# Staging the weight sums of a seven-product up-projection, with new priorities for evictions, squares and residual steps

## The chip, the cores and the metric

The kernel runs on one NeuronCore of a Trainium2 chip. The metric is the device time of one execution in microseconds (us). TensorE (PE in the profile) multiplies, VectorE (DVE), ScalarE (ACT) and GpSimd (POOL) do elementwise work, and SyncE's queue (SP) issues the DMAs. Each engine runs its own queue in order: an instruction that waits holds back everything behind it on the same engine.

## The reference, cut to what matters

The computation is a trunk of two layers, a gated DeltaNet and an mLSTM mixer, each followed by a causal convolutional feed-forward block (ConvFFN). There are 1040 tokens of width 1024 (16 learned meta tokens ahead of 1024 frames). Every sub-layer is normed before and after and is added to the residual stream:

```python
def conv_ffn(h, w_up, conv_w, conv_b, w_down):
    u = causal_depthwise_conv(h @ w_up, conv_w) + conv_b
    gate, up = u[..., :FFN_DIM], u[..., FFN_DIM:]
    return (jax.nn.silu(gate) * up) @ w_down
...
for i in range(DEPTH):
    a_in = rms_norm(hs, norm_w[i, 0])
    mix = gated_deltanet(a_in, ...) if i % 2 == 0 else mlstm(a_in, ...)
    hs = hs + keep * rms_norm(mix, norm_w[i, 1])
    f = conv_ffn(rms_norm(hs, norm_w[i, 2]), ffn_w_up[i], ffn_conv_w[i], ffn_conv_b[i], ffn_w_down[i])
    hs = hs + keep * rms_norm(f, norm_w[i, 3])
```

All is float32. FFN_DIM is 2816, that is 22 column tiles of 128 for the gate and 22 for the up half.

## The kernel before, in words

**Precision.** Every large product is made of three fast matmuls (`mm3`, lines 233 to 235): a weight is split into a high and a low part, and so is the activation, and high·high, high·low and low·high are accumulated. The split of one weight tile of 128x512 (`split_slot`, line 129) is a cast on ACT (line 137) and a subtraction on POOL (line 138). Split weights live in ten slots of the tag `w`, so in five pairs; raw weights in nine slots of the tag `raw`.

**Tokens.** The 1040 tokens are two halves of 520 (`t`), each of two quarters of 260 (`n`).

**The up-projection** (`up`, line 1238) works on one tile `j` at a time: 128 gate columns and 128 up columns. It has two forms.
- Plain (four weight tiles, `plain`, line 180): for the first half of the tokens, for j from 0 to 5. Four groups of 24 matmuls; each result is copied out of PSUM by ACT (line 1250).
- Seven products (`quad`, line 162): the 2x2 block product (two row blocks of the weight by two column blocks; two quarters of tokens) in the Strassen-Winograd form. Seven products of 12 matmuls take the place of eight. The weight side needs four sums of 128x512 tiles on DVE: s1 (line 171), s3 (line 174), s2 (line 175), s4 (line 177). s2 overwrites the raw tile of a11, and s4 that of s2, so each must wait until the split before it has been read by POOL. The seven weights are used in the order a11, s2, s3, s1, s4, a22, a12. After each product `combine` (line 194) folds the PSUM bank into temporaries and results: an ACT copy for product 0 (line 203), DVE adds for the others (line 196, by the profile), which free the bank.

The order of tiles (`ffn_plan`, line 1285) is: six plain tiles for the first half; then j = 6 to 11 for both halves ("pair" tiles, 14 products), each followed by tile j - 6 for the second half alone ("single" tiles, 7 products); then j = 12 to 21 as pairs. After a tile's products, the causal convolution (ACT line 1276, DVE line 1278), the SiLU (ACT line 1280), the gate product (POOL line 1281) and a store follow.

**Weights ahead.** `next_quad` (line 187) is called at the start of each tile. It loads and prepares the next tile's weights (as long as fewer than seven weight tiles are ready ahead), then hands over the current tile's. So the whole of `quad` for tile T+1, its four DMAs, four sums and seven splits, is issued ahead of the products of tile T.

**Norms and residual.** A down or output projection (`second`, line 386) accumulates in SBUF (DVE lines 439 and 441) and, in its last group, sums squares over the features (`squares`, line 284: ACT line 294, DVE line 295). `post` (line 334) then loads the old residual stream, norms the result (a matmul with ones on PE, line 302, and Ln and Exp on ACT, lines 262 and 265), scales it (DVE line 352), adds it to the stream (DVE line 353), stores it, and sums the squares for the next norm. It is put off by `later` and run by `tick`, that is after a set amount of PE work. The norm's matmul keeps its program place on PE. `ffn_operands` (line 1183) then scales the new stream (DVE line 1206) and makes the activation side of the seven products (casts on ACT line 1212, DVE lines 1213 and 1217).

**What sets the order.** The builder orders each engine's queue when the program is compiled. What is issued earlier in the program has precedence; `high_priority(300)` gives an instruction the precedence of one issued 300 instructions earlier; an ordering edge (`order`) forces one instruction behind another on its engine. Before the change, `combine` and the accumulations have 300 (the accumulations of a last group 3000), and the copies of plain tiles, the squares and `post` have nothing.

Of the kernel before, what the change touches and what calls it, by code (L numbers as in the profile page):

```python
# [12 lines left out]
ALU = mybir.AluOpType  # L13
# [16 lines left out]
QB = HB // 2  # L30
# [2 lines left out]
N_RAW, N_SPLIT = 9, 10  # L33

W_AHEAD = 7

N_PAGES = 19

# [4 lines left out]
LAG_POST, LAG_N, LAG_PRE, LAG_OPS = 6, 6, 16, 2  # L43

LAST = ("f1", 1)
# [31 lines left out]
def run(g):  # L77
    for _ in g:
        pass


class Trunk:
# [5 lines left out]
    def page(self, tag, name, bufs, dt=F32):  # L88
        return self.pool.tile([P, BS], dt, tag=tag, name=name, bufs=bufs)
# [72 lines left out]
    def quad(self, src, name):  # L162

        a11, a21, a22, a12, s1 = [self.raw_slot(f"{name}_{i}") for i in range(5)]
        for t, q in ((a21, 2), (a22, 3), (a11, 0), (a12, 1)):
            self.nc.sync.dma_start(t, src(q))
        v = self.nc.vector
        split = lambda t, n: self.split_slot(t, f"{name}_{n}")  # L170
        v.tensor_tensor(s1, a21, a22, ALU.add)
        w = [split(a11, "a11")]
        s3, s2, s4 = a21, a11, a11
        v.tensor_tensor(s3, a11, a21, ALU.subtract)
        v.tensor_tensor(s2, s1, a11, ALU.subtract)
        w += [split(s2, "s2"), split(s3, "s3"), split(s1, "s1")]
        v.tensor_tensor(s4, a12, s2, ALU.subtract)
        return w + [split(s4, "s4"), split(a22, "a22"), split(a12, "a12")]

    def plain(self, src, name):  # L180

# [4 lines left out]

    def next_quad(self):

        while self.quads and (not self.ready or sum(len(w) for w in self.ready[1:]) < W_AHEAD):
            make, *args = self.quads.pop(0)  # L190
            self.ready.append(make(*args))
        return self.ready.pop(0)

    def combine(self, i, ps, tmp, out):

        add = lambda o, u: self.nc.vector.tensor_tensor(o, ps[:, :QB], u, ALU.add)  # L196
        m1, u2, u3 = tmp
        with self.tc.high_priority(300):
            self.combine_now(i, ps, add, m1, u2, u3, out)

    def combine_now(self, i, ps, add, m1, u2, u3, out):
        if i == 0:
            self.nc.scalar.copy(m1, ps[:, :QB])
        elif i == 1:
            add(u2, m1)
        elif i == 2:
            add(u3, u2)
        elif i == 3:
            add(out[3], u3)
            add(u2, u2)  # L210
        elif i == 4:
            add(out[1], u2)
        elif i == 5:
            add(out[2], u3)
        else:
            add(out[0], m1)

    def temps(self, name):
        return [self.page(tag, f"{n}_{name}", 2)[:, :QB] for n, tag in (("m1", "part"), ("u2", "rs"), ("u3", "sum"))]
# [63 lines left out]

    def squares(self, pages, name, acc=None):

        nc = self.nc
        n = pages[0].shape[1]
        for m, p in enumerate(pages):
            if acc is None:
                acc = self.page("sum", f"ss_{name}", 2)[:, :n]  # L290
                nc.scalar.activation(acc, p, AF.Square)
                continue
            sq = self.scratch(f"sq_{name}_{m}")[:, :n]
            self.last_square = nc.scalar.activation(sq, p, AF.Square)  # L294
            nc.vector.tensor_tensor(acc, acc, sq, ALU.add)  # L295
        return acc
# [37 lines left out]
    def post(self, t, n, acc, mix, post, pre, name, direct, then):  # L334


        nc = self.nc
        q = 2 * t + n
        sl = slice(q * QB, (q + 1) * QB)
        old, src, rt = self.hs, self.new_hs, self.new_rt  # L340

        def job():
            hs = []
            c = 4 if name[0] == "f" or t == 0 else 2
            for g in range(KD // c):
                h = self.fp_page(f"hs_{name}_{q}_{g}") if c == 4 else self.raw_input(f"hs_{name}_{q}_{g}")
                nc.sync.dma_start(h, old[:, c * g : c * g + c, sl])
                hs.append(h)
            page = lambda m: hs[m // c][:, m % c]
            r = self.norm(acc, f"o{name}{q}")  # L350
            for m in range(KD):
                nc.vector.scalar_tensor_tensor(mix[m], mix[m], self.nw[:, post, m : m + 1], r, ALU.mult, ALU.mult)  # L352
                (nc.gpsimd if pre is None and m % 2 else nc.vector).tensor_tensor(page(m), page(m), mix[m], ALU.add)  # L353
                if direct:
                    self.put_input(page(m), m, sl)
            if pre is None:
                t0 = max(NMETA - q * QB, 0)
                o0 = q * QB + t0 - NMETA
                out = self.a["out"].rearrange("(m p) t -> p m t", p=P)
                for m in range(0, KD, 2):  # L360
                    nc.sync.dma_start(out[:, m : m + 2, o0 : o0 + QB - t0], hs[m // c][:, m % c : m % c + 2, t0:])
                return
            for g, h in enumerate(hs):
                nc.sync.dma_start(src[:, c * g : c * g + c, sl], h)
            acc2 = self.squares([page(m) for m in range(KD)], f"{name}{q}")

            def factors():
                self.norm(acc2, f"{name}{q}", rt[:, sl])
                if then:
                    self.later(LAG_OPS, lambda: then(src, rt))  # L370

            self.later(LAG_PRE, factors)

        self.later(LAG_POST + (0 if (name, t) == LAST else n * LAG_N), job)

    def next_stream(self, name, pre):

# [860 lines left out]
    def up(self, L, j, halves):  # L1238

        nc = self.nc  # L1240
        w = self.next_quad()
        tmp = {t: self.temps(f"u{L}_{j}_{t}") for t in halves if len(w) == 7}
        u = {(t, i, n): self.page("C", f"u_{L}_{j}_{t}_{i}_{n}", N_PAGES) for t in halves for n in range(2) for i in range(2)}
        if len(w) == 4:
            for h in range(2):
                for n in range(2):
                    ps = self.next_bank(f"up_{L}_{j}_{h}_{n}")[:, :QB]
                    for k in range(KD):
                        self.mm3(ps, [z[:, k % 4] for z in w[2 * h + k // 4]], self.xplain(k, n), k == 0, k == KD - 1)
                    nc.scalar.copy(u[0, h, n][:, 2 : 2 + QB], ps)  # L1250
                    self.tick(4)
        for i in range(7) if len(w) == 7 else ():
            for t in halves:
                ps = self.next_bank(f"up_{L}_{j}_{t}_{i}")
                for k in range(4):
                    self.mm3(ps[:, :QB], [z[:, k] for z in w[i]], self.xo[t](i, k), k == 0, k == 3)
                self.combine(i, ps, tmp[t], [u[t, h, n][:, 2 : 2 + QB] for h in range(2) for n in range(2)])
                self.tick(2)
        for t in halves:
            y = {}  # L1260
            for n in range(2):
                for h in range(2):
                    p = u[t, h, n]
                    if t + n == 0:
                        nc.gpsimd.memset(p[:, :2], 0.0)
                    elif n == 0 and len(halves) == 1:
                        nc.gpsimd.tensor_copy(p[:, :2], self.ftail[:, j, h])
                    else:
                        nc.gpsimd.tensor_copy(p[:, :2], u[t - (1 - n), h, 1 - n][:, QB : QB + 2])
                    if t == 0 and n == 1 and len(halves) == 1:  # L1270
                        nc.gpsimd.tensor_copy(self.ftail[:, j, h], p[:, QB : QB + 2])
                    y[h] = self.page("C", f"y_{L}_{j}_{t}_{h}_{n}", N_PAGES)[:, :QB]
                    tt = h * NF + j
                    taps = self.fcw[:, tt, :]
                    z = self.bank(("pp", "px")[h], f"z_{L}_{j}_{t}_{h}_{n}")[:, :QB]
                    nc.scalar.activation(z, p[:, 2 : 2 + QB], AF.Identity, scale=taps[:, 2:3], bias=self.fcb[:, tt : tt + 1])  # L1276
                    for i in (1, 0):
                        nc.vector.scalar_tensor_tensor(z if i or not h else y[h], p[:, i : i + QB], taps[:, i : i + 1], z, ALU.mult, ALU.add)  # L1278
                    if h == 0:
                        nc.scalar.activation(y[0], z, AF.Silu)  # L1280
                nc.gpsimd.tensor_tensor(y[0], y[0], y[1], ALU.mult)
                c0 = t * HB + n * QB
                nc.sync.dma_start(self.hidden[:, j, c0 : c0 + QB], y[0])
# [214 lines left out]
```

## Time and profile before

| | us |
|---|---|
| median of 3 runs (3446.24 to 3463.75) | 3447.37 |
| the profiled execution, device time | 3444.23 |
| span of its instructions | 3442.5 |
| PE busy | 3212.2 |
| DVE busy | 2373.1 |
| POOL busy | 1652.2 |
| ACT busy | 1609.0 |

The span is the time from the first to the last instruction; the device time has 1.7 us around it. Busy times are unions over the span. PE's clock is also read in the profile: the share of full speed that was granted to it, 0.969 over the whole span. A matmul's end is modelled, so where PE is busy all the time it may still wait for nothing but its own pipeline. In the waits view, a row names the waiting engine and line, what it waited for, the total in us, how often, and the longest.

By the views over stretches, the gated DeltaNet and most of its output projection take the first 1290 us, the plain tiles of the first ConvFFN begin at 1353 us, the seven-product tiles run from 1461 to 1865 us and the down-projection until about 2150 us; in the second ConvFFN the plain tiles begin at 2649 us and the seven-product tiles run from 2755 to 3162 us.

### The profile page before, as it was taken

The page shows a single profiled execution, that of the slowest core. Times are in us where ns is not written, and L with a number is a line of the kernel's source. Part 1 is how long each engine was busy: PE and PEld are TensorE (multiplying, and loading weights), DVE is VectorE, ACT ScalarE, POOL GpSimd, SP SyncE. Part 2 cuts the span into 40 slices and gives each one's busy share as a digit, 9 for nine tenths or more (in the row PEclk, how much of TensorE's full clock was granted, in tenths as well). Part 3 has the DMA queues.
Part 4 walks back from the last instruction along what each step waited for, and adds up shares of the span by engine and source line. Part 5 has one row for each costly group of instructions (what it writes and reads, how often), then busy time and mean ns, then how long its engine had stood idle before and what let it go on. Part 6 is the DMA issues. An engine that isn't in the chain of part 4 may idle for free. (4 is left out here: it accounts for less than half of the span.)

```text
span 3442.5 us, 68429 instructions
## 1 busy us (share of the span) xinstructions
PE 3212.2 (93%) x25368; PEld 3119.6 (91%) x25368; DVE 2373.1 (69%) x5143; ACT 1609.0 (47%) x3390; POOL 1652.2 (48%) x1890
## 2 busy tenths in 40 slices
PE   7999999999999998799999989899998799999998
PEld 6889988988988897799999989899998799999998
DVE  7777777777767649877677484534469867777474
ACT  5455545555545435655455243323345645445232
POOL 2433443444334444577665434333344477666453
PEclk9999999999999999899999999999999899999999
DMA  3011100101001344422224453211125422224452
GB/s 118 23 37 34 34 29 31 34 32 34 31 31 40 107 132 152 134 93 93 78 78 133 133 182 125 93 44 50 56 78 183 136 90 87 87 75 132 132 180 88
DMA packets 234511, 297.75 MB, mean 86 GB/s; under 512 B 20684, under 2 KB 167104, under 8 KB 234176
## 3 DMA queue, kind: packets, MB, share of 16 engines
q1 hardware_dynamic: 234176, 293.37, 26.3%
q8 instruction: 200, 3.28, 0.4%
q14 instruction: 135, 1.11, 0.1%
HBM read 240.06 MB, written 53.23 MB: 85 GB/s over the span
## 5 line engine op out<-in xcount | busy, mean ns | idle before, releaser
L233 PE MATMUL pj_gi<-xh_in,wh_gi 128*128 128x348 f32 x1152 | 394.2, 342 | 5.5 <-ACT wh_gi L137 3.7
L233 PE MATMUL dn_f<-so_f,wh_f 128*128 128x260 f32 x1344 | 386.6, 288 | 11.8 <-ACT wh_f L137 5.0
L235 PE MATMUL pj_gi<-xh_in,wl_gi 128*128 128x348 f32 x1152 | 395.7, 343 | 0.9 <-POOL wl_gi L138 0.9
L234 PE MATMUL pj_gi<-xl_in,wh_gi 128*128 128x348 f32 x1152 | 393.5, 342 | 0.0
L235 PE MATMUL dn_f<-so_f,wl_f 128*128 128x260 f32 x1344 | 384.7, 286 | 0.0
L234 PE MATMUL dn_f<-so_f,wh_f 128*128 128x260 f32 x1344 | 384.5, 286 | 0.0
L138 POOL TENSOR_TENSOR wl_f<-wr_f,wh_f 128x512 fp32r<-128x512 f32 x168 | 226.0, 1362 | 246.0 <-ACT wh_f L137 113.5
L1278 DVE SCALAR_TENSOR_TENSOR z<-u,fcw,z 128x260 f32<-128x260 f32 x528 | 243.4, 487 | 49.8 <-ACT z L1276 35.0
L138 POOL TENSOR_TENSOR wl_u_s<-wr_u,wh_u_s 128x512 fp32r<-128x512 f32 x176 | 228.2, 1300 | 97.7 <-ACT wh_u_s L137 97.3
L233 PEld LDWEIGHTS dn_f<-so_f,wh_f 128*128 128x128 f32 x1344 | 257.7, 192 | 13.6 <-ACT z L1276 5.5
L441 DVE TENSOR_TENSOR acc_f<-acc_f,dn_f 128x260 f32<-128x260 f32 x320 | 133.1, 421 | 189.2 <-PE dn_f L235 188.2
L234 PEld LDWEIGHTS dn_f<-so_f,wh_f 128*128 128x128 f32 x1344 | 258.2, 192 | 0.2
L235 PEld LDWEIGHTS dn_f<-so_f,wl_f 128*128 128x128 f32 x1344 | 258.2, 192 | 0.1
L1276 ACT ACTIVATE z<-u,fcb,fcw 128x260 f32<-128x260 f32 x352 | 192.3, 570 | 93.7 <-DVE u L196 92.4
L233 PEld LDWEIGHTS pj_gi<-xh_in,wh_gi 128*128 128x128 f32 x1152 | 222.1, 193 | 8.0 <-ACT wh_gi L137 4.0
L235 PEld LDWEIGHTS pj_gi<-xh_in,wl_gi 128*128 128x128 f32 x1152 | 222.6, 193 | 2.4 <-POOL wl_gi L138 1.2
L234 PEld LDWEIGHTS pj_gi<-xl_in,wh_gi 128*128 128x128 f32 x1152 | 222.2, 193 | 0.7 <-issue 0.2
L138 POOL TENSOR_TENSOR wl_gi<-wr_gi,wh_gi 128x512 fp32r<-128x512 f32 x96 | 132.4, 1380 | 157.8 <-ACT wh_gi L137 153.8
L137 ACT CAST wh_u_s<-wr_u 128x512 fp32r<-128x512 f32 x176 | 105.9, 615 | 192.5 <-PE up L234 134.9
L697 DVE SCALAR_TENSOR_TENSOR gy<-u_g,c_gdn_conv_w_g,gy 128x348 f32<-128x348 f32 x288 | 187.9, 663 | 7.9 <-ACT gy L695 5.4
L138 POOL TENSOR_TENSOR wl_u_a<-wr_u,wh_u_a 128x512 fp32r<-128x512 f32 x132 | 170.1, 1293 | 37.0 <-ACT wh_u_a L137 36.3
L137 ACT CAST wh_f<-wr_f 128x512 fp32r<-128x512 f32 x168 | 103.1, 617 | 178.8 <-PE dn_f L234 133.0
(501 smaller groups left out, 11718.0 us busy)
## 6 DMA issues: line engine op xcount, KB each, us to landing
wr_u<-in_ffn_w_up_dram SPq DMA_DIRECT2D x224, 256.0 KB, 2.6
wr_f<-in_ffn_w_down_dram SPq DMA_DIRECT2D x176, 256.0 KB, 2.8
wr_gi<-in_gdn_w_in_dram SPq DMA_DIRECT2D x96, 256.0 KB, 2.6
h<-y SPq DMA_DIRECT2D x176, 130.0 KB, 2.3
si_f<-h SPq DMA_DIRECT2D x88, 260.0 KB, 3.5
wr_go<-in_gdn_w_out_dram SPq DMA_DIRECT2D x64, 256.0 KB, 2.7
wr_mi<-in_ml_w_in_dram SPq DMA_DIRECT2D x44, 256.0 KB, 2.6
o_g<-gy SPq DMA_DIRECT2D x48, 174.0 KB, 1.8
```

The source lines that it names most:

```text
L137: nc.scalar.copy(hi, part(raw))
L138: nc.gpsimd.tensor_tensor(lo, part(raw), hi.bitcast(F32), ALU.subtract)
L233: nc.tensor.matmul(out, w[0], x[0], start=start, stop=False)
L234: nc.tensor.matmul(out, w[0], x[1], start=False, stop=False)
L235: nc.tensor.matmul(out, w[1], x[0], start=False, stop=stop)
L441: nc.vector.tensor_tensor(acc[m][n], acc[m][n], ps, ALU.add)
L697: ins = nc.vector.scalar_tensor_tensor(y, u[:, j : j + BS], taps[:, j : j + 1], y, ALU.mult, ALU.add)
L1276: nc.scalar.activation(z, p[:, 2 : 2 + QB], AF.Identity, scale=taps[:, 2:3], bias=self.fcb[:, tt : tt + 1])
L1278: nc.vector.scalar_tensor_tensor(z if i or not h else y[h], p[:, i : i + QB], taps[:, i : i + 1], z, ALU.mult, ALU.add)
```

## The change: what it does, and its diff

Four things change.
- **`quad` in stages.** The first part still comes at the start of tile T, ahead of its products: the four loads, s1, s3 and the split of a11. The second (s2 and the splits of s2, s3, s1) is issued after product 3 of tile T, the third (s4 and the splits of s4, a22, a12) after product 5. Both sums get an ordering edge behind the last `combine` of that product. In a plain tile the stages are issued after its first and its second column block, without an edge. `next_quad` issues whatever is left before it hands a tile over, and counts an unfinished quad as seven weight tiles.
- **Plain copies** (line 1250) get `high_priority(300)`.
- **`squares`** gets `high_priority(300)` wherever it is called.
- **`post`'s job** gets `high_priority(300)`: its loads, norm, scaling, adds, stores and squares. (The squares inside it thereby have both offsets.) The later job, the norm for the next sub-layer, has none.

`combine` now returns its last instruction; what it computes, and in which order, is the same. Products, sums, splits and loads are the same in number and size.

```diff
+S2_BEHIND, S4_BEHIND = 3, 5
...
 def quad(self, src, name):
...
         split = lambda t, n: self.split_slot(t, f"{name}_{n}")
+        s3, s2, s4 = a21, a11, a11
         v.tensor_tensor(s1, a21, a22, ALU.add)
-        w = [split(a11, "a11")]
-        s3, s2, s4 = a21, a11, a11
         v.tensor_tensor(s3, a11, a21, ALU.subtract)
-        v.tensor_tensor(s2, s1, a11, ALU.subtract)
-        w += [split(s2, "s2"), split(s3, "s3"), split(s1, "s1")]
-        v.tensor_tensor(s4, a12, s2, ALU.subtract)
-        return w + [split(s4, "s4"), split(a22, "a22"), split(a12, "a12")]
+        w = Weights([split(a11, "a11")])
+
+        def second(behind):
+            ins = v.tensor_tensor(s2, s1, a11, ALU.subtract)
+            if behind:
+                self.order(ins, behind)
+            w.extend([split(s2, "s2"), split(s3, "s3"), split(s1, "s1")])
+
+        def third(behind):
+            ins = v.tensor_tensor(s4, a12, s2, ALU.subtract)
+            if behind:
+                self.order(ins, behind)
+            w.extend([split(s4, "s4"), split(a22, "a22"), split(a12, "a12")])
+
+        w.stages = [(S2_BEHIND, second), (S4_BEHIND, third)]
+        return w
+
+    def stage(self, i, behind=None):
+
+        for w in self.ready:
+            stages = getattr(w, "stages", [])
+            while stages and stages[0][0] <= i:
+                stages.pop(0)[1](behind)
...
     def next_quad(self):
 
-        while self.quads and (not self.ready or sum(len(w) for w in self.ready[1:]) < W_AHEAD):
+        if self.ready:
+            self.stage(7)
+        while self.quads and (not self.ready or sum(7 if getattr(w, "stages", ()) else len(w) for w in self.ready[1:]) < W_AHEAD):
             make, *args = self.quads.pop(0)
             self.ready.append(make(*args))
+            if len(self.ready) == 1:
+                self.stage(7)
         return self.ready.pop(0)
...
     def squares(self, pages, name, acc=None):
 
+        with self.tc.high_priority(300):
+            return self.squares_now(pages, name, acc)
...
-        self.later(LAG_POST + (0 if (name, t) == LAST else n * LAG_N), job)
+        def first_job():
+            with self.tc.high_priority(300):
+                job()
+
+        self.later(LAG_POST + (0 if (name, t) == LAST else n * LAG_N), first_job)
...
-                    nc.scalar.copy(u[0, h, n][:, 2 : 2 + QB], ps)
+                    with self.tc.high_priority(300):
+                        nc.scalar.copy(u[0, h, n][:, 2 : 2 + QB], ps)
                     self.tick(4)
+                self.stage((S2_BEHIND, S4_BEHIND)[h])
...
-                self.combine(i, ps, tmp[t], [u[t, h, n][:, 2 : 2 + QB] for h in range(2) for n in range(2)])
+                last = self.combine(i, ps, tmp[t], [u[t, h, n][:, 2 : 2 + QB] for h in range(2) for n in range(2)])
                 self.tick(2)
+            self.stage(i, last)
```

More of the change, by code (lines that the diff above doesn't have):

```diff
@@ L79, in run @@
         pass
+class Weights(list):
+    stages = ()
 class Trunk:
@@ L198, in combine @@
         with self.tc.high_priority(300):
-            self.combine_now(i, ps, add, m1, u2, u3, out)
+            return self.combine_now(i, ps, add, m1, u2, u3, out)
     def combine_now(self, i, ps, add, m1, u2, u3, out):
         if i == 0:
[L203 to L208, printed above, removed]
-            add(out[3], u3)
[L210 to L216, printed above, removed]
+            return self.nc.scalar.copy(m1, ps[:, :QB])
+        if i == 3:
+            add(out[3], u3)
+        o, u = ((u2, m1), (u3, u2), (u2, u2), (out[1], u2), (out[2], u3), (out[0], m1))[i - 1]
+        return add(o, u)
     def temps(self, name):
@@ L284, in squares, with squares_now @@
     def squares(self, pages, name, acc=None):
+        with self.tc.high_priority(300):
+            return self.squares_now(pages, name, acc)
+    def squares_now(self, pages, name, acc):
         nc = self.nc
```

## The prediction

> **What bounds the kernel now.** I read the page's busy times first, then the waits of PE, then the timelines of DVE and ACT around the waits that repeat, and last the stretches with their granted clock.
>
> ```profile
> span 3442.5 us, 68429 instructions
> ...
> PE 3212.2 (93%) x25368; PEld 3119.6 (91%) x25368; DVE 2373.1 (69%) x5143; ACT 1609.0 (47%) x3390; POOL 1652.2 (48%) x1890
> ```
>
> PE is busy in 3212.2 of 3442.5 us, and the change takes no matmul away. It can pay only in PE's idle 230 us and in the time at a lowered clock. Who ends that idle time, over the whole span (total us, times, longest):
>
> ```profile
> PE px L923 <- DVE Z L920: 46.5, 40, 2.7
> PE up L233 <- DVE u L196: 21.5, 12, 1.8
> PE up L233 <- ACT u L1250: 17.4, 7, 6.8
> PE fs_f L302 <- DVE ss_f L295: 17.0, 4, 6.4
> PE fs_go L302 <- DVE ss_go L295: 16.2, 4, 5.3
> PE fs_mo L302 <- DVE ss_mo L295: 14.9, 4, 5.2
> ```
>
> The first row is the DeltaNet's inverse, which the change doesn't touch. The other five are what its four parts aim at: combines (21.5), plain copies (17.4), and norms that wait for sums of squares (48.1). Here is DVE around one of the twelve waits of the second row, which ended at 1527.6 us, at the end of a single tile:
>
> ```profile
> 1521.70 1.22 DVE L175 TENSOR_TENSOR wr_u<-wr_u,wr_u 128x512 f32<-128x512 f32 x1 [0.51 <-POOL wl_u_a L138]
> 1522.84 0.47 DVE L1278 SCALAR_TENSOR_TENSOR y<-u,fcw,z 128x260 f32<-128x260 f32 x1
> 1523.24 0.41 DVE L196 TENSOR_TENSOR u<-up,u_u 128x260 f32<-128x260 f32 x1
> 1523.58 0.41 DVE L196 TENSOR_TENSOR u_u<-up,u_u 128x260 f32<-128x260 f32 x1
> 1525.48 1.74 DVE L177 TENSOR_TENSOR wr_u<-wr_u,wr_u 128x512 f32<-128x512 f32 x1 [1.49 <-POOL wl_u_s L138]
> 1527.14 0.75 DVE L196 TENSOR_TENSOR u<-up,u_u 128x260 f32<-128x260 f32 x2
> 1527.82 0.41 DVE L196 TENSOR_TENSOR u<-up,m_u 128x260 f32<-128x260 f32 x1
> ```
>
> After the two adds of product 3, DVE's next in line is s4 (L177) for the next tile. It stands 1.49 us until POOL has read s2, then runs 1.74 us. Only then come two combines at once, the second late: PE's banks are full, and PE waits for them. That is a wait in a queue, not a lack of DVE time.
>
> **The staged sums.** It removes no instruction; s2 moves behind product 3's combine and s4 behind product 5's. What the gaps cost is read from stretches that begin and end at the matmul after a gap (columns: length; PE, PEld, DVE, ACT, POOL busy; granted clock; DMA):
>
> ```profile
> 1494.92:1560.28 65.36, 61.43 (x505) 60.66 (x505) 48.21 (x107) 33.87 (x71) 50.34 (x65) 1.00 0.27 90
> 1560.28:1662.90 102.62, 96.71 (x757) 95.54 (x757) 72.71 (x160) 51.13 (x106) 75.55 (x97) 0.95 0.26 86
> 1662.90:1690.00 27.10, 27.10 (x213) 27.10 (x214) 19.61 (x47) 14.64 (x31) 18.71 (x27) 0.94 0.24 79
> 2789.22:2960.18 170.96, 161.17 (x1261) 159.26 (x1261) 121.45 (x266) 85.21 (x176) 125.81 (x161) 0.95 0.26 86
> 2960.18:2987.28 27.10, 27.10 (x213) 27.10 (x214) 19.65 (x47) 14.62 (x31) 18.74 (x27) 0.94 0.23 79
> ```
>
> The first row holds two periods of a pair and a single tile, 32.68 us each at full clock; the second holds three of 34.21 us, the fourth five of 34.19 us, at 0.95. So in eight periods a gap of 1.8 us costs 1.5 us more through the clock, and after the last gap of each block (0.94 of 27.1 us) 1.6 us: 8 x 1.52 + 2 x 1.6 = 15.4 us. With the 21.5 us of idle time the gaps cost 36.9 us.
>
> [...]
>
> Do the sums stop blocking? A period of 32.68 - 1.8 = 30.9 us holds 21 products of 12 matmuls, 1.47 us each; in a pair tile a product takes two of these. The other prices:
>
> ```profile
> L138 POOL TENSOR_TENSOR wl_u_s<-wr_u,wh_u_s 128x512 fp32r<-128x512 f32 x176 | 228.2, 1300 | 97.7 <-ACT wh_u_s L137 97.3
> ...
> L1281 POOL TENSOR_TENSOR y<-y,y 128x260 f32<-128x260 f32 x176 | 137.3, 784 | 55.6 <-DVE y L1278 39.0 <-ACT y L1280 11.3 <-issue 3.7
> ...
> L137 ACT CAST wh_u_s<-wr_u 128x512 fp32r<-128x512 f32 x176 | 105.9, 615 | 192.5 <-PE up L234 134.9 <-DVE wr_u L177 31.6 <-DVE wr_u L175 25.9
> ```
>
> In a single tile s2 now runs after product 3's combine (up to 1.74 us), its cast takes 0.62 and POOL 1.30: 3.7 us, while s4 stands behind product 5, 2 x 1.47 = 2.9 us after product 3. So s4 may still wait some 0.8 us and run 1.74, but only product 6's combine is behind it. PE has four banks here, so it can run three more products (4.4 us) before it needs that one; 0.8 + 1.74 = 2.5 us is covered. In pair tiles s4 stands 5.9 us after product 3 and needn't wait. I take the whole gain, **-37 us** (bounds: -37, and 0 if the wait only moves). What is behind the new edges on DVE's queue is later combines and the convolution's taps, both under that cover. The new weights are needed late: s2 at product 1 of the next tile, in the tightest order (single, then pair) 3 x 1.47 + 2.94 = 7.35 us after product 3, against 3.7 us of work. The loads stay where they are.
>
> **Copies, squares and post at the entry of each ConvFFN.** One wait of 6.8 us for a copy, from ACT's queue:
>
> ```profile
> 1421.09 0.39 ACT L1280 ACTIVATE y<-z 128x260 f32<-128x260 f32 x1 [1.29 <-DVE z L1278]
> 1423.37 0.62 ACT L1212 CAST t_go<-f_b_go 128x520 fp32r<-128x520 f32 x1 [1.89 <-DVE f_b_go L1217]
> 1423.90 0.92 ACT L1250 COPY u<-up 128x260 f32<-128x260 f32 x3
> ```
>
> Copies of finished banks stood behind a SiLU and a cast that waited for DVE; with 300 they come first. But the stretches of the two entries show a ceiling for such gains:
>
> ```profile
> 1280.00:1450.00 170.00, 135.73 (x1019) 131.82 (x1018) 153.67 (x286) 98.66 (x207) 78.05 (x79) 0.91 0.50 160
> 2560.00:2730.00 170.00, 136.55 (x1008) 131.30 (x1007) 155.00 (x293) 97.03 (x203) 71.39 (x64) 0.90 0.52 165
> ```
>
> PE is idle 34 us in each and loses 0.09 to 0.10 of 170 us, 15 to 17 us, to the clock, some 50 us; DVE is busy 153.7 and 155.0 of 170. Residual steps, squares and operands are one DVE chain that PE must wait for, and priorities change its order, not its sum. What the norms gain ahead of 1353 us, the first operands give back. Each stretch can shorten by DVE's idle time at most, 16.3 and 15.0 us. The copies are ACT's and lie at the end, where the chain is nearly through, so I take 10 us each: **-20 us** (bounds: -31, and 0). Post's loads and stores come ahead of weight loads on SP, and a store that waits for its add holds these back; plain tiles are fetched two ahead, 2 x 96 matmuls or 23 us (by 1.47 us for 12), which covers it. On POOL, post has adds only in the last block, spread over the down-projection.
>
> **Squares and post at the end of the first ConvFFN**, where two halves are normed into the mLSTM (17.0 us above):
>
> ```profile
> 2000.00:2060.00 60.00, 51.38 (x387) 50.53 (x386) 51.50 (x104) 30.53 (x61) 22.11 (x20) 0.91 0.56 181
> 2150.00:2215.00 65.00, 53.47 (x314) 49.38 (x313) 48.08 (x105) 27.78 (x64) 23.82 (x18) 0.92 0.32 104
> ```
>
> Among the sums of squares that quarter 0's norm waits for, from 2019.5 to 2027.2 us, DVE also ran:
>
> ```profile
> L352 DVE SCALAR_TENSOR_TENSOR acc_f<-acc_f,c_norm_w_g,rs_of 128x260 f32<-128x260 f32 x4 | 2.9, 732 | 0.0
> ```
>
> DVE has 8.5 and 16.9 us idle in the two stretches, so order can pay. Those scalings, 2.9 us, are mostly quarter 1's; the squares' doubled offset puts them behind, and I assume the same for the second stretch. I take 3 us for each quarter 0, 1 us for each quarter 1, and of the clock's loss (0.09 x 60 + 0.08 x 65 = 10.6 us) 4 us: **-12 us** (bounds: -27.6, and 0).
>
> **At the start** `squares` now goes ahead of the splits of the first input, for which PE waits (second row; the first is the tail's):
>
> ```profile
> PE fs_of L302 <- DVE ss_of L295: 3.6, 1, 3.6
> ...
> PE pj_ggdn L234 <- DVE xl_in L332: 2.4, 2, 2.1
> ```
>
> A few squares between the splits: **+1 us** (bounds 0 and, if the wait doubles, +2.4; the norm that gains stands behind 24 matmuls that hide it anyway). At the tail post and squares move alike and keep their order; if they didn't, the first row's 3.6 us would go or double. I take 0.
>
> **Sum:** -37 - 20 - 12 + 1 = -68 us against the profiled execution's 3444.2, so 3376; against the median of 3447.4 it is **3379 us**.
>
> **The rivals.**
> - *Waits only change places* at entries and ends: the DVE-bound stretches take back what copies and norms gain. For it: DVE's 90% there. Against: 17.4 us of copies were behind work that itself waited. The staged sums alone: 3447 - 37 = 3410 us.
> - *s4 blocks again* behind product 5, because POOL is later than I think. For it: L177's 1.49 us wait was POOL's. Against: the four banks. Then the other parts alone: 3447 - 31 = 3416 us.
> - *A gap costs only itself*, the clock falling for other reasons: 3379 + 15 = 3394 us. Ten of twelve gaps speak against it. [...]
> - *All of it*: bounds reached, 37 + 31 + 28 = 96 us: 3351 us.
> - *Nothing moves*: the builder's order was set by readiness, not precedence, and the same instructions stand first: 3447 us. For it: combines had 300 already and still came second. Against: an edge is no precedence.
> - *Slower: late weights.* The second and third stages let PE run into a weight that isn't split. It decides from the point where more than 7.35 - 3.7 = 3.6 us of other POOL work stands ahead of s2's split, that is two further splits and a gate product (2 x 1.30 + 0.78 = 3.4) and a little more. Price: a split of 1.30 us and 1.53 us of clock at each of 44 tiles, 124.5 us: 3379 + 125 = 3504 us.
>
> **How the numbers follow.** Forecast 0.43; waits change places 0.22; s4 again 0.10; gap only 0.03; all of it 0.10; nothing 0.06; late weights 0.06. A difference of 0.5%, 17.2 us, is about what a measurement of this kernel can tell from no change: 3430 and 3465 us are the bounds. Forecast, first, third and fourth rival and nearly all of the second are faster (0.86); nothing and the rest of the second are the same (0.08); late weights are slower (0.06). The range reaches from 3338, a little beyond the bounds, to 3428, above the second rival; it leaves out the last two.
>
> **What would show it.** Staged sums: the row of `up` waiting for L196 (21.5, 12) is gone, the periods of pair and single tile are near 30.9 us at clock 1.00, and L177 has combines of product 5 ahead of it. Copies: the longest wait for L1250 is under 2 us. Squares and post: the waits of `fs_` for L295 fall from 48.1 us by about a quarter; if the first operands (L1212) wait longer instead, the first rival holds. Wrong would be waits of `up` for ACT L137 or POOL L138, which are next to nothing now, or gaps of 1.8 us that remain.

## The result, and the profile after

| | us |
|---|---|
| before, median of 6 runs (3438.74 to 3463.75) | 3446.91 |
| after, median of 6 runs (3409.05 to 3422.82) | 3412.97 |
| ratio, with its 95% interval | 0.990 (0.9875 to 0.9925) |
| the profiled execution of after, device time | 3414.69 |

The change makes the kernel 1.0% faster, 34 us. The prediction said 68 us: the direction is right, and the size is half of that. The page of after:

```profile
span 3412.7 us, 68346 instructions
...
PE 3197.3 (94%) x25368; PEld 3109.4 (91%) x25368; DVE 2361.2 (69%) x5143; ACT 1594.1 (47%) x3384; POOL 1662.0 (49%) x1890
```

First the seven-product tiles, from their first matmul to the first of the down-projection, in the first and in the second ConvFFN. The stretches of before and then of after (columns: length; PE, PEld, DVE, ACT, POOL busy; granted clock; DMA):

```profile
1460.90:1865.60 404.70, 391.82 (x3194) 389.28 (x3192) 290.28 (x650) 206.28 (x425) 282.93 (x378) 0.98 0.28 92
2755.30:3162.80 407.50, 394.91 (x3194) 392.45 (x3193) 291.97 (x651) 206.40 (x425) 283.57 (x377) 0.97 0.28 91
```

```profile
1466.60:1850.50 383.90, 382.64 (x3195) 382.46 (x3193) 288.63 (x652) 203.54 (x426) 290.24 (x378) 1.00 0.30 96
2743.70:3128.20 384.50, 383.10 (x3194) 382.89 (x3192) 287.60 (x650) 203.62 (x426) 291.14 (x378) 1.00 0.30 96
```

PE is idle for 1.3 and 1.4 us there, where it was idle for 12.9 and 12.6, and the clock is full. The two blocks are 20.8 and 23.0 us shorter, 43.8 us, more than the whole change brings. DVE's queue at the end of a single tile shows why (compare the DVE timeline in the prediction; adds of product 3, s2, adds of products 4 and 5, of product 6, s4):

```profile
1525.50 0.42 DVE L227 TENSOR_TENSOR u_u<-up,u_u 128x260 f32<-128x260 f32 x1
1525.83 1.14 DVE L186 TENSOR_TENSOR wr_u<-wr_u,wr_u 128x512 f32<-128x512 f32 x1
1526.89 0.75 DVE L227 TENSOR_TENSOR u<-up,u_u 128x260 f32<-128x260 f32 x2
1527.56 0.41 DVE L227 TENSOR_TENSOR u<-up,m_u 128x260 f32<-128x260 f32 x1
1529.11 0.69 DVE L192 TENSOR_TENSOR wr_u<-wr_u,wr_u 128x512 f32<-128x512 f32 x1 [1.13 <-POOL wl_u_s L146]
```

s4 (L192) still waits for POOL, 1.13 us, but no combine of the tile stands behind it any more.

So 10 us by the medians, 14 us by the profiled executions (spans 3442.5 and 3412.7 us), were lost elsewhere. PE's waits after the change (total us, times, longest):

```profile
PE pj_gi L255 <- DVE grow_gdn L334: 16.9, 1, 16.9
PE dn_go L255 <- DVE acc_go L471: 12.5, 4, 5.2
PE dn_f L255 <- DVE acc_f L469: 11.2, 10, 3.7
PE dn_mo L255 <- DVE acc_mo L469: 10.6, 4, 4.9
PE up L255 <- ACT u L1281: 9.1, 4, 3.2
PE fs_f L328 <- DVE ss_f L321: 8.9, 2, 4.7
PE up L255 <- ACT b_go L1242: 6.0, 1, 6.0
PE up L255 <- ACT b_mo L1242: 5.4, 1, 5.4
...
PE fs_mo L328 <- ACT u L1281: 5.0, 1, 5.0
PE fs_go L328 <- ACT u L1281: 4.5, 1, 4.5
...
PE fs_go L328 <- DVE ss_go L321: 2.4, 1, 2.4
...
PE fs_mo L328 <- DVE ss_mo L321: 2.4, 1, 2.4
```

The row of `up` for the combines (21.5 us, 12 times) is gone. The norms' waits for sums of squares fell from 48.1 to 13.7 us. But the output and down-projections now wait for their own accumulations (34.3 us), the first operands (`b_go`, `b_mo`) come later, and two norms stand behind plain copies. Before, the rows of these kinds that the prediction doesn't show were small:

```profile
PE up L233 <- ACT b_go L1212: 4.0, 2, 3.6
PE up L233 <- ACT b_mo L1212: 4.0, 2, 3.6
...
PE dn_f L233 <- DVE acc_f L441: 2.2, 1, 2.2
...
PE dn_go L233 <- DVE acc_go L441: 2.1, 2, 1.8
```

Added up with four more rows of 1.4 us or less (4.3 us), the norms ahead of the sub-layers, copies, first operands and accumulations made PE wait 82.1 us before. After, the eleven rows above (all but the first) and three more of 1.4 us or less (3.9 us) make 81.9. Three priorities moved these waits about and left their sum as it was. The norms of the projections' own results (`fs_ogo`, `fs_omo`, `fs_of`) fell from 8.3 to 3.5 us beside that, and the 16.9 us of the first row are new.

Where the time went, stage by stage, by the starts of the same matmuls, counted in PE's order, in each trace (us against before; the runs of the last four columns are told below):

| stage, its length before | after | sums alone | priorities alone | input squares plain | accumulations first |
|---|---|---|---|---|---|
| start, to the first inverse, 95.7 | +8.5 | -1.1 | +8.3 | +0.7 | -2.8 |
| DeltaNet, 1176.9 | +0.1 | -3.7 | -0.3 | +0.3 | -4.2 |
| its output projection, 80.1 | +5.5 | +1.8 | +7.8 | +5.6 | -0.2 |
| plain tiles, 108.3 | -8.4 | -1.5 | -7.8 | -7.6 | -2.0 |
| seven-product tiles, 404.7 | -20.8 | -20.0 | +2.3 | -20.8 | -19.8 |
| down-projection, mLSTM, 696.0 | +2.1 | +0.8 | -0.9 | +1.5 | +1.4 |
| its output projection, 87.1 | +7.3 | +0.5 | +7.6 | +7.6 | +2.9 |
| plain tiles, 106.5 | -5.8 | +0.5 | -5.1 | -6.8 | -1.2 |
| seven-product tiles, 407.5 | -23.0 | -23.7 | -1.3 | -23.8 | -22.9 |
| last down-projection and norm, 268.3 | +4.7 | +1.1 | +2.1 | +5.3 | +0.1 |
| all | -29.8 | -45.5 | +12.8 | -38.0 | -48.8 |

The DeltaNet's row, in which nothing is changed, differs by up to 4 us from build to build; less than that is not read as an effect in any row.

From this came the theory for the experiments: the staged sums bring the whole gain, some 44 us; the priorities only move waits at the entries and ends, and cost 8.5 us at the start. The rivals: the prediction's own terms (the priorities bring 31 us), and that the parts need each other.

### The profile page after: what moved, and what is told of

It is laid out like the page before. It is cut to its first block, busy times and chain, and to the rows that moved or that the text cites. A ratio compares the mean times of both kernels' runs of the same rounds, so it can differ in the third digit from the quotient of the medians.

```text
span 3412.7 us, 68346 instructions
## 1 busy us (share of the span) xinstructions
PE 3197.3 (94%) x25368; PEld 3109.4 (91%) x25368; DVE 2361.2 (69%) x5143; ACT 1594.1 (47%) x3384; POOL 1662.0 (49%) x1890
## 4 chain that ended last, share of the span: by engine, by line
PE 72%; DVE 14%; issue 2%; ACT 2%; DMA 2%; POOL 1%; SPq 0%; POOLq 0%; DVEq 0%; ACTq 0%
PE up L255 8%; PE up L257 8%; PE up L256 8%; PE dn_f L255 5%; PE dn_f L257 5%; PE dn_f L256 5%; PE pj_gi L257 4%; PE pj_gi L256 3%; PE pj_gi L255 3%; PE pj_mi L255 2%; PE pj_mi L256 2%; PE pj_mi L257 2%; PE pp L979 1%; PE px L993 1%; PE px L988 1%
## 5 line engine op out<-in xcount | busy, mean ns | idle before, releaser
L255 PE MATMUL pj_gi<-xh_in,wh_gi 128*128 128x348 f32 x1152 | 393.2, 341 | 18.1 <-DVE grow_gdn L334 16.9
L255 PE MATMUL dn_f<-so_f,wh_f 128*128 128x260 f32 x1344 | 386.7, 288 | 23.2 <-DVE acc_f L469 11.2
L146 POOL TENSOR_TENSOR wl_u_s<-wr_u,wh_u_s 128x512 fp32r<-128x512 f32 x176 | 245.8, 1400 | 77.9 <-ACT wh_u_s L145 77.2
```

The lines of the kernel that those rows point to most:

```text
L146: nc.gpsimd.tensor_tensor(lo, part(raw), hi.bitcast(F32), ALU.subtract)
L255: nc.tensor.matmul(out, w[0], x[0], start=start, stop=False)
```

## The experiments

All ratios are to before, with 95% intervals.

**1. The staged sums alone.** The changed kernel with its three priorities undone:

```diff
     def squares(self, pages, name, acc=None):
-        with self.tc.high_priority(300):
-            return self.squares_now(pages, name, acc)
+        return self.squares_now(pages, name, acc)
...
-        self.later(LAG_POST + (0 if (name, t) == LAST else n * LAG_N), first_job)
+        self.later(LAG_POST + (0 if (name, t) == LAST else n * LAG_N), job)
...
-                    with self.tc.high_priority(300):
-                        nc.scalar.copy(u[0, h, n][:, 2 : 2 + QB], ps)
+                    nc.scalar.copy(u[0, h, n][:, 2 : 2 + QB], ps)
```

> The staged sums without any of the three priorities. By the ledger of the two traces (each part acts in its own place): the seven-product tiles shorten by the same 20.9 and 23.5 us as in the changed kernel and nothing else moves, so 44 us less than before, about 3403 us, which is faster than the whole change. By the prediction's term: 37 us less, 3410 us. Rival (the tiles gain only because copies and squares reach them earlier): less than 30 us, over 3417 us.

Measured: 3400.1 us, ratio 0.988 (0.986 to 0.990). The tiles gain what they gain with the whole change (the table's third column), and the norms wait as before:

```profile
PE fs_f L327 <- DVE ss_f L320: 17.0, 4, 6.4
...
PE fs_go L327 <- DVE ss_go L320: 16.0, 4, 6.1
PE fs_mo L327 <- DVE ss_mo L320: 14.0, 4, 5.0
```

The sums don't need the priorities.

**2. The priorities alone.** The kernel before with the three edits above the other way round.

> The three priorities without the staged sums. By the ledger: 8.5 us lost at the start, 5.5 and 7.2 us at the two output projections, 4.8 us at the last down-projection, 8.4 and 5.8 us gained in the plain tiles, so some 10 to 15 us slower than before, about 3460 us, and the 1.8 us waits of the seven-product tiles for the combines are there as before. By the prediction's terms: 31 us faster, 3416 us. Rival (the priorities are neutral, and the staging itself costs what is lost elsewhere): within 3 us of before.

Measured: 3457.5 us, ratio 1.0035 (1.0022 to 1.0048): a loss, as the table's stages said. Some of PE's waits:

```profile
PE up L233 <- DVE u L196: 21.6, 12, 1.8
PE pj_gi L233 <- DVE grow_gdn L312: 16.9, 1, 16.9
PE dn_go L233 <- DVE acc_go L449: 14.2, 5, 5.7
```

The old wait is there, and so are the new ones. The prediction's 31 us for these parts are refuted.

**3. The first input's squares plain again.**

```diff
-            acc = self.squares(hs[b], f"in{b}")
+            acc = self.squares_now(hs[b], f"in{b}", None)
```

> The changed kernel with the squares of the first input at their old precedence; all else as changed. By the ledger: the wait of 16.9 us of the first projection for its scaling goes back to under 1 us, the first gate matmul comes 9.5 us earlier, and the whole is 8 to 9 us shorter than the changed kernel, about 3404 us. Rival (the wait at the start is another's, for instance for the splits on ACT): the same as the changed kernel, 3413 us.

Measured: 3402.1 us, ratio 0.9874 (0.9859 to 0.9889), and the wait is back to nothing:

```profile
PE pj_gi L255 <- DVE grow_gdn L334: 0.8, 1, 0.8
```

What had happened at the start is seen in DVE's timeline. Before, the first scaling, which frees a PSUM bank, ran as soon as the norm was there:

```profile
19.64 0.51 DVE L308 TENSOR_TENSOR grow_gdn<-pj_ggdn,r_in 32x348 f32<-32x348 f32 x1 [0.25 <-ACT r_in L265]
```

After, the squares of all three token blocks and the splits among them stood ahead of it. These are the last of them, and then the scaling:

```profile
27.39 4.77 DVE L321 TENSOR_TENSOR ss_in<-ss_in,sq_in 128x348 f32<-128x348 f32 x5
32.08 4.02 DVE L358 SCALAR_TENSOR_TENSOR xl_in<-hs_in,c_norm_w_g,xh_in 128x348 fp32r<-128x348 f32 x8
36.02 0.50 DVE L334 TENSOR_TENSOR grow_gdn<-pj_ggdn,r_in 32x348 f32<-32x348 f32 x1
```

**4. Sums and copies.** As the first experiment, with the copies' precedence kept.

> Staged sums and the copies' precedence, without squares and post. By the ledger, if the plain tiles' 8.4 and 5.8 us come from the copies: 44 + 14 = 58 us less than before, about 3389 us. If they come from squares and post having done the work ahead of the plain tiles already (work that only changed places): as the sums alone, about 3403 us.

Measured: 3400.9 us, ratio 0.987 (0.9854 to 0.9886), the same as the sums alone. The copies bring nothing of their own: PE still waits 16.9 us for them in all (17.4 before), only in shorter pieces (4.8 us at most, where it was 6.8).

**5. Which of the two sums blocks.** The sums alone, without the edge of s2:

```diff
         def second(behind):
-            ins = v.tensor_tensor(s2, s1, a11, ALU.subtract)
-            if behind:
-                self.order(ins, behind)
+            v.tensor_tensor(s2, s1, a11, ALU.subtract)
```

> Staged sums alone, as in the run of the sums alone (3400 us), but without the ordering edge of s2; s4 keeps its own. In the built DVE queue of a single tile s2 then stands ahead of product 3's adds again, as before the change, and s4 behind product 5's. If s4's wait in the queue is what blocked (the prediction's diagnosis): no waits of 1.8 us, 3400 us within 5. Rival (s2, which runs ahead of the two adds of product 3, is as much to blame): six waits of about 1 us or more in each seven-product block, 3415 us or more.

Measured: 3431.0 us, ratio 0.9958 (0.9940 to 0.9976): the rival holds. s2 is the other half of the wait. It runs ahead of product 3's adds and itself waits for POOL (DVE's timeline, then PE's, then the first block):

```profile
1517.41 1.22 DVE L186 TENSOR_TENSOR wr_u<-wr_u,wr_u 128x512 f32<-128x512 f32 x1 [1.03 <-POOL wl_u_a L146]
...
1518.95 0.42 DVE L225 TENSOR_TENSOR u<-up,u_u 128x260 f32<-128x260 f32 x1
1519.29 0.41 DVE L225 TENSOR_TENSOR u_u<-up,u_u 128x260 f32<-128x260 f32 x1
```

```profile
1519.85 0.36 PE L253 MATMUL up<-b_go,wh_u_a 128*128 128x260 f32 x1 [1.17 <-ACT wh_u_s L145]
```

```profile
1456.10:1855.00 398.90, 386.59 (x3195) 383.71 (x3193) 290.28 (x650) 204.61 (x426) 285.12 (x378) 1.00 0.28 93
```

PE goes on 0.15 us after product 3's second add has ended (1519.29 + 0.41 = 1519.70); the view names a cast of the same moment, and I read the wait as one for the bank. The waits are now 1.2 and 0.6 us long, twelve in the first block, and the clock stays at 1.00. That point comes back at the end.

**6. Staging without edges.**

```diff
-            self.stage(i, last)
+            self.stage(i)
```

> Staged sums alone, with both ordering edges left out: the sums are still issued behind products 3 and 5, and the combines keep their 300. In the built DVE queue of a single tile the order is then s2, adds of product 3, s4, adds of products 4 to 6, word for word that of before. If the order on DVE is the whole cause: the twelve waits of 1.8 us come back with their half-clock windows, 3440 to 3447 us. Rival (issuing later is what helps, since the splits on ACT and POOL move too): at most 3415 us.

Measured: 3445.2 us, ratio 0.9997 (0.9983 to 1.0012), no change that can be told. All 5143 instructions of DVE ran in the order of before, and the wait is back:

```profile
PE up L255 <- DVE u L227: 21.6, 12, 1.8
```

Issuing the sums later is worth nothing by itself; the gain comes with the two ordering edges. (Of the prediction's rivals, "nothing moves" is what happens without them.) Whether a precedence of the combines above 300 would do the same as the edges wasn't tried.

**7. Accumulations first.** Experiment 3, and the projections' accumulations ahead of squares and residual steps:

```diff
-                    with self.tc.high_priority(3000 if last else 300):
+                    with self.tc.high_priority(3000 if last else 900):
```

> The changed kernel with plain squares of the first input (3402 us), and with the accumulations of the projections at a precedence of 900 instead of 300, ahead of squares and residual steps. If the waits only change places: the waits of the projections for their accumulations (12.3 and 11.1 us at the output projections, 9.6 us at the down-projections) fall to under 8 us in all, the norms' waits for sums of squares rise from 14 us towards the 47 us that they have with the sums alone, and the time stays at 3402 us within 4. Rival (the accumulations were merely sorted badly against squares): both waits stay small, 3380 to 3390 us.

Measured: 3397.1 us, ratio 0.9857 (0.9833 to 0.9880). The waits of the projections (33.0 us in experiment 3) are 4.7 us in all, and the norms wait again:

```profile
PE fs_f L328 <- DVE ss_f L321: 15.0, 4, 4.6
...
PE fs_mo L328 <- DVE ss_mo L321: 9.9, 3, 5.1
PE fs_go L328 <- DVE ss_go L321: 9.8, 3, 5.2
```

The norms ahead of the sub-layers, copies, first operands and accumulations together cost PE 81.8 us here, 80.5 us in experiment 1, 81.9 us after the change, 82.1 us before. This is the fastest of the kernels that leave nothing out, but its interval overlaps with that of the sums alone.

**8. Half of the residual adds on POOL.** On the sums alone, to see whether DVE's work or its order sets the pace:

```diff
-                (nc.gpsimd if pre is None and m % 2 else nc.vector).tensor_tensor(page(m), page(m), mix[m], ALU.add)
+                (nc.gpsimd if m % 2 else nc.vector).tensor_tensor(page(m), page(m), mix[m], ALU.add)
```

> The sums alone (3400 us), with every second residual add of every quarter on POOL instead of DVE; the same sums are computed. Each quarter takes four adds of about 0.4 us off DVE, 6 us for four quarters, at each of the three places. If DVE's work, not its order, sets the end there: the norms' waits (47.0 us) fall by 12 us or more, and with the clock the time falls by 10 to 18 us, to 3382 to 3390 us. Rival (the adds wait for POOL, which is slower at 0.78 us each and has weight splits of 1.3 us queued): no gain or a loss, 3400 to 3410 us.

Measured: a median of 3412.5 us, but with a wide spread (3403.3 to 3425.4), ratio 0.9902 (0.9877 to 0.9927); its profiled execution, the shortest of the six, has a span of 3401.4 us against 3397.2 of the sums alone. No gain. From the first output projection to the last plain tile, the groups of DVE and the stretch with the sums alone:

```profile
L466 DVE TENSOR_TENSOR acc_go<-acc_go,dn_go 128x260 f32<-128x260 f32 x49 | 20.1, 414 | 1.8 <-PE dn_go L257 1.7
L377 DVE SCALAR_TENSOR_TENSOR acc_go<-acc_go,c_norm_w_g,rs_ogo 128x260 f32<-128x260 f32 x32 | 19.1, 627 | 1.1 <-ACT rs_ogo L287 1.1
...
L378 DVE TENSOR_TENSOR hs_go<-hs_go,acc_go 128x260 f32<-128x260 f32 x32 | 15.4, 510 | 0.0
```

```profile
1267.70:1456.30 188.60, 156.55 (x1170) 152.51 (x1169) 164.50 (x308) 108.83 (x231) 88.87 (x94) 0.91 0.49 153
```

and with half of the adds on POOL:

```profile
L377 DVE SCALAR_TENSOR_TENSOR acc_go<-acc_go,c_norm_w_g,rs_ogo 128x260 f32<-128x260 f32 x32 | 22.5, 733 | 0.0
L466 DVE TENSOR_TENSOR acc_go<-acc_go,dn_go 128x260 f32<-128x260 f32 x49 | 20.2, 415 | 2.9 <-PE dn_go L257 2.8
...
L378 DVE TENSOR_TENSOR hs_go<-hs_go,acc_go 128x260 f32<-128x260 f32 x16 | 9.8, 612 | 0.0
```

```profile
1267.90:1455.00 187.10, 154.72 (x1171) 150.79 (x1170) 167.77 (x290) 108.58 (x231) 102.33 (x110) 0.92 0.49 154
```

Sixteen adds have left DVE (15.4 to 9.8 us), and DVE is busier than before (164.5 to 167.8 us): the scalings (L377) take longer on the mean (627 to 733 ns), and the accumulations (L466) don't (414 and 415 ns). Taken one by one in the two stretches, no scaling that ran without a POOL instruction beside it took more than 489 ns (43 of 64), and the 21 that overlapped with one took 1.1 us on average. An accumulation took at most 427 ns, with POOL at work or not. The scalings of the two entries in the trace of before (L352) show the same: 47 of 64 had no POOL instruction beside them and took at most 490 ns, the other 17 took 1.1 us on average.

**9. The norm's matmul later.** On the sums alone:

```diff
-LAG_POST, LAG_N, LAG_PRE, LAG_OPS = 6, 6, 16, 2
+LAG_POST, LAG_N, LAG_PRE, LAG_OPS = 6, 6, 24, 2
```

> The sums alone (3400 us), with the norm's matmul of the next sub-layer put 24 instead of 16 units of PE work behind the residual step. A unit is six matmuls, so 0.72 us at 0.12 us each: 5.7 us later. If PE waits there only because the norm's matmul keeps its program place ahead of matmuls that could run: its waits for sums of squares (fs_go, fs_mo, fs_f: 47.0 us, at most 6.4 us each) fall by half or more, and the time by 15 us or more, to 3385 us or less. If DVE's work sets the end (the prediction's ceiling): the waits turn up at the first operands, the copies and the first mLSTM projections, 3400 us within 5.

Measured: 3402.1 us, ratio 0.9876 (0.9854 to 0.9898), as the sums alone. The norms' waits for squares fall from 47.0 to 33.0 us, and 20.6 us turn up elsewhere, at norms that find the copies not done:

```profile
PE fs_mo L327 <- ACT u L1275: 10.3, 1, 10.3
PE fs_go L327 <- ACT u L1275: 10.3, 1, 10.3
```

So the norms' early place in PE's program is not why PE waits there.

**10. Less work for DVE.** On the sums alone; the residual add is left out, so this kernel computes something else, and the scaled result takes the place of the stream:

```diff
-                nc.vector.scalar_tensor_tensor(mix[m], mix[m], self.nw[:, post, m : m + 1], r, ALU.mult, ALU.mult)
-                (nc.gpsimd if pre is None and m % 2 else nc.vector).tensor_tensor(page(m), page(m), mix[m], ALU.add)
+                nc.vector.scalar_tensor_tensor(page(m), mix[m], self.nw[:, post, m : m + 1], r, ALU.mult, ALU.mult)
```

> The sums alone (3400 us), with the residual add left out: the scaled result takes the place of the stream, and all that follows still waits for the norm. This leaves out eight adds per quarter (15.4 us of DVE in the stretch from the output projection to the last plain tile) without giving POOL more to do. If DVE's work sets the end of these stretches: each of the two shortens by 12 to 20 us with its clock, the end of the first ConvFFN by some 5 and the tail by some 3, 3355 to 3370 us. Rival (the place of the norm's matmuls on PE, and the chain of one quarter after another, set it): under 6 us for each stretch, 3385 us or more.

Measured: 3369.9 us, ratio 0.9779 (0.9756 to 0.9801). The two stretches, and the second one with the sums alone:

```profile
1270.50:1447.50 177.00, 150.77 (x1170) 148.10 (x1169) 154.20 (x274) 108.72 (x231) 87.12 (x94) 0.94 0.51 163
2528.10:2712.30 184.20, 158.46 (x1206) 155.05 (x1205) 162.05 (x290) 112.83 (x239) 87.69 (x96) 0.94 0.52 165
```

```profile
2537.80:2732.50 194.70, 161.83 (x1206) 156.99 (x1206) 171.62 (x323) 113.46 (x239) 92.45 (x96) 0.91 0.50 157
```

The first is 11.6 us shorter than with the sums alone (188.6), the second 10.5 (184.2 against 194.7). DVE is busy for 154.2 us, 10.3 less, in the first, and for 162.1 us, 9.6 less, in the second. The gain of a stretch is about what DVE is spared, a little under the 12 to 20 us that were expected. Priorities, lags and a second engine had moved the same stretches by some 3 us at most. Leaving the add out also takes a link out of the chain from a norm to the next squares; this run can't tell that from DVE's busy time.

## Why the prediction was half right, point by point

- **What bounds the kernel, and the ceiling at the entries: right.** The prediction said that the entries are one DVE chain, and that priorities change its order and not its sum. Experiments 7 to 10 show it. But the step after that, "The copies are ACT's and lie at the end, where the chain is nearly through, so I take 10 us each", went against it and failed. The entries (output projection and plain tiles) changed by -2.9 and +1.5 us, not by -20 in all, and experiment 4 shows the copies to be worth nothing alone. The 50 us of idle time and clock that the prediction found in each entry counts some time twice: of the 15 to 17 us put to the clock, 10.4 and 10.3 us fell on time in which PE was busy, and in the rest PE was idle anyway.
- **The staged sums: right in place and mechanism, 37 us forecast, 43.8 measured.** Idle time fell by 22.8 us (12.9 + 12.6 to 1.3 + 1.4; forecast 21.5). Ten periods of 3.41 us at half clock (0.50 granted) are gone, 17.1 us (forecast 15.4, worked out from stretches). Of PE's modelled busy time 3.9 us more went. The diagnosis was incomplete: the prediction put the blame on s4 alone, and in experiment 5, without s2's edge, two thirds of the gain are gone (s2's edge without s4's wasn't tried). The rival "s4 blocks again" did not come: s4 waits 1.13 us (0.8 forecast), but behind product 6's combine too, so that nothing is held up.
- **Squares and post at the end of the first ConvFFN: -12 forecast, +2.1 measured** for the whole stage. "DVE has 8.5 and 16.9 us idle in the two stretches, so order can pay" is the failed step: the norms' wait fell from 17.0 to 8.9 us, and waits for accumulations (L469), of which this stage had none before, took 6.9 of their 11.2 us there.
- **The start: +1 forecast, +8.5 measured.** "A few squares between the splits" missed that an instruction with 300 also passes the scalings of the projections, which had 300 already and came later in the program. They free the PSUM banks; PE stood 16.9 us for them.
- **The tail: 0 forecast, +4.7 measured in the last stage.** This is little more than builds differ by: experiments 4 and 5, in which `squares` and `post` are those of before, have +3.5 and +3.3 there. The waits for accumulations rose from 2.2 to 4.4 us in this stage; what else the 4.7 us hold stays open.
- **The sum.** With 43.8 and 8.5 put in, and nothing for entries and ends, it is -35 us; the medians differ by 34, the profiled executions by 30. The rival "waits only change places" (3410 us, 3 us from the result) tells what happened to three of the four parts, and the prediction gave it half the chance of the forecast. That its number comes so near is in part luck: it has 37 us for the sums and nothing for the start, where the runs show 43.8 and 8.5. Its sign was named there and came: the first operands wait longer (8.0 to 11.4 us). The longest wait for a copy is 3.2 us in the products and 5.0 us at a norm, not under 2.

What is left open: why the DeltaNet's stage differs by up to 4 us between builds in which it is the same, and why the gain of experiment 10 is a little under the 15.4 us of adds that were left out.

## What to carry to other kernels

Before pricing a priority, ask of the engine in question how much of the stretch it is busy: at the 87 to 90% of these entries a priority picked who waits, and only work taken off that engine shortened the stretch. Where a queue has idle time and an instruction in it waits, its place is worth fixing. Here it took an ordering edge behind the instruction that must go first; a later issue, with a precedence of 300 on the combines, left the queue as it was. And list what already had the same precedence further on in the program, since a raised instruction passes that too.

## What the runs showed of the hardware

**Ten of twelve gaps of 1.8 us were followed by half clock.** In the trace of before, PE has six such gaps in each of the two blocks of seven-product tiles. After the last four of the first block and all six of the second, a period of 3.41 us at a granted clock of 0.50 began 0.9 to 1.4 us after PE had gone on. The first and the last of the ten (columns as above):

```profile
1561.63:1565.04 3.41, 3.41 (x18) 3.41 (x18) 2.64 (x8) 2.89 (x8) 2.91 (x5) 0.50 0.44 142
2961.09:2964.51 3.42, 3.42 (x18) 3.42 (x17) 2.65 (x7) 2.94 (x8) 3.12 (x5) 0.50 0.29 104
```

After the first two gaps of the first block the clock stayed at 1.00; what sets these two apart stays open. After the change, without the gaps, the clock is 1.00 in both blocks. The twelve waits of 0.6 to 1.2 us in the first block of experiment 5 left it at 1.00 too.

**Work moved from DVE to POOL slowed DVE down** by more than it had been spared: 16 adds fewer (5.6 us), and 3.3 us more of busy time (164.5 to 167.8 us, experiment 8). The scalings took 733 ns on the mean where they had taken 627, the accumulations 415 ns where they had taken 414.
